# Splitting the first load of a streaming softmax into two transfers of 64 partitions

## The chip, the cores and the metric

The kernel runs on one core of a Trainium2 chip. The metric is device time in microseconds (us): lower is better. The core has the engines VectorE (DVE in the profile), ScalarE (ACT), GpSimd (POOL), TensorE (PE, not used here) and SyncE (SP), and 16 DMA engines that move data between DRAM and the on-chip memory SBUF, which has 128 partitions.

## The reference

A softmax over the last axis of a float32 tensor of 16 x 1024 x 512, that is, 16384 rows of 512 numbers, 33.55 MB in and 33.55 MB out.

```python
x_max = np.max(x, axis=-1, keepdims=True)
exp_x = np.exp(x - x_max)
return (exp_x / np.sum(exp_x, axis=-1, keepdims=True)).astype(np.float32)
```

## The kernel before

The 16384 rows are seen as 128 row sets of 128 rows, one row of each set in each partition. The row sets are moved in eight blocks of 16 (`BLOCKS`): block (0, 16) is the first 2048 rows of the input, and partition p takes 16 neighbouring rows of it, 32 KB in one piece of DRAM. So each of the eight loads ("L" in `ORDER`) and of the eight stores ("S") moves 4.19 MB over all 128 partitions. SBUF holds a ring of 96 row sets (`RING`), called `held`; the softmax is computed in place there.

Computing goes in 16 groups of eight row sets, two groups to a block. For each group g:

- VectorE takes the negated maximum of the eight rows of each partition (`rowmax`, M0 to M15 in the list `VECTOR`, line 164). Before the first group of a block it waits for the load's semaphore (`take(nc.vector, loaded[k], 16)`, through the helper on line 110). A transfer adds 16 to its semaphore when all of it has landed.
- ScalarE takes exp(x - max) of one row at a time and sums it (line 195, eight activations a group, in a loop over the groups). It preloads its table on line 188.
- VectorE takes reciprocals of the sums (line 170), and GpSimd (P0 to P11) or VectorE (V12 to V15) multiplies the rows by them (line 172).

Both the order of VectorE's steps (`VECTOR`) and the order of the transfers (`ORDER`) are written out by hand. All transfers are issued by SyncE, in the order of `ORDER`. The first six loads (`AHEAD`) are issued at once, without a wait (lines 124 to 136, through `load` on line 125). Behind them, SyncE waits for the two multiplies of a block before it stores it (line 152), and for the store of a block before it loads another one into its place in the ring. At the end SyncE waits for the last stores.

The program starts with an entry barrier of all engines (line 223 of a library file in the profile), and a second one stands between the six loads and the rest (line 137). When the program is finalized, `loads_at_the_head` moves the first load that SyncE issues from behind the entry barrier to ahead of it:

```python
AT_HEAD = {mybir.EngineType.SP: 1}
...
        loads = [
            i
            for i in body.instructions
            if i.engine == engine and type(i).__name__ == "InstDMACopy"
        ][:count]
...
        main.instructions[barrier:barrier] = loads
```

The count is in instructions: one DMA instruction of SyncE goes ahead of the barrier. In the list of the loads, that is all of load 0.

Of the kernel before, what the change touches and what calls it, by code (L numbers as in the profile page):

```python
# [1 line left out]

# [4 lines left out]

F32 = mybir.dt.float32
EXP = mybir.ActivationFunctionType.Exp
AX = mybir.AxisListType.X  # L10

GROUP = 8
GROUPS = 16
RING = 12 * GROUP

BLOCKS = [(0, 16), (16, 32), (32, 48), (48, 64), (64, 80), (80, 96), (96, 112), (112, 128)]
ORDER = [
    ("L", (0, 16)),
    ("L", (16, 32)),
    ("L", (32, 48)),
    ("L", (48, 64)),
    ("L", (64, 80)),
    ("L", (80, 96)),
    ("S", (0, 16)),
    ("S", (16, 32)),  # L30
    ("S", (32, 48)),
    ("L", (96, 112)),
    ("L", (112, 128)),
    ("S", (48, 64)),
    ("S", (64, 80)),
    ("S", (80, 96)),
    ("S", (96, 112)),
    ("S", (112, 128)),
]
AHEAD = 6  # L40

VECTOR = """
    M0 M1 P0 M2 P1 M3 P2 M4 P3 M5 P4 M6 P5 M7 P6 M8 P7 M9 P8 M10 P9 M11
    P10 M12 P11 M13 V12 M14 V13 M15 V14 V15
"""

AT_HEAD = {mybir.EngineType.SP: 1}

def loads_at_the_head(nc):

    main, body = nc.main_func.blocks[0], nc.main_func.blocks[1]
    for engine, count in AT_HEAD.items():
# [5 lines that stand above are left out]
        barrier = next(  # L62
            n
            for n, i in enumerate(main.instructions)
            if i.engine == engine and type(i).__name__ == "InstDrain"
        )
        for load in loads:
            body.instructions.remove(load)
        main.instructions[barrier:barrier] = loads


@with_exitstack
def kernel(
    ctx: ExitStack,
    tc: tile.TileContext,
    x: bass.AP,
    out: bass.AP,
):
    nc = tc.nc
    nc.at_finalize(loads_at_the_head)  # L80
    P = nc.NUM_PARTITIONS

    d = x.shape[-1]
    x_rows, out_rows = x.flatten_outer_dims(), out.flatten_outer_dims()
    assert x_rows.shape[0] == GROUPS * GROUP * P

    def in_dram(rows, a, b):

        first, last = next(k for k in BLOCKS if k[0] <= a and b <= k[1])
        block = rows[first * P : last * P].rearrange("(p r) d -> p r d", p=P)  # L90
        return block[:, a - first : b - first, :]

    held = nc.alloc_sbuf_tensor("held", [P, RING, d], F32).ap()
    shift = nc.alloc_sbuf_tensor("shift", [P, GROUPS * GROUP], F32).ap()
    sums = nc.alloc_sbuf_tensor("sums", [P, GROUPS * GROUP], F32).ap()
    recip = nc.alloc_sbuf_tensor("recip", [P, GROUPS * GROUP], F32).ap()

    loads = [k for what, k in ORDER if what == "L"]
    stores = [k for what, k in ORDER if what == "S"]
    loaded = {k: nc.alloc_semaphore(f"loaded{k[0]}") for k in loads}  # L100
    scaled = [nc.alloc_semaphore(f"scaled{g}") for g in range(GROUPS)]
    stored = {k: nc.alloc_semaphore(f"stored{k[0]}") for k in stores}
    maxed = nc.alloc_semaphore("maxed")
    expd = nc.alloc_semaphore("expd")
    to_pool = nc.alloc_semaphore("to_pool")
    to_vector = nc.alloc_semaphore("to_vector")

    def take(engine, semaphore, n):

        engine.wait_ge(semaphore, n).then_inc(semaphore, -n)  # L110

    def rows(a, b):
        assert a // RING == (b - 1) // RING
        return held[:, a % RING : (b - 1) % RING + 1, :]

    def meets(k, a, b):
        return k[0] < b and a < k[1]

    def group(g):
        return g * GROUP, (g + 1) * GROUP  # L120

    def stats(t, g):
        return t[:, g * GROUP : (g + 1) * GROUP]

    def load(k):
        copy = nc.sync.dma_start(out=rows(*k), in_=in_dram(x_rows, *k))
        copy.then_inc(loaded[k], 16)
        return copy

    with tc.manual_schedule():
        for _, k in ORDER[:AHEAD]:
            tc.no_tile_sem_insts.add(load(k).ins.name)
    tc.close()
    tc.compile()  # L137

    taken, done = set(), set()
    for what, k in ORDER[AHEAD:]:  # L140
        if what == "L":
            for s in stores:
                if meets(s, k[0] - RING, k[1] - RING) and s not in taken:
                    take(nc.sync, stored[s], 16)
                    taken.add(s)
            load(k)
        else:
            for g in range(GROUPS):
                if meets(k, *group(g)) and g not in done:
                    take(nc.sync, scaled[g], 1)  # L150
                    done.add(g)
            nc.sync.dma_start(out=in_dram(out_rows, *k), in_=rows(*k)).then_inc(
                stored[k], 16
            )


    seen = set()

    def rowmax(g):
        for k in loads:  # L160
            if meets(k, *group(g)) and k not in seen:
                take(nc.vector, loaded[k], 16)
                seen.add(k)
        nc.vector.reduce_max(  # L164
            out=stats(shift, g), in_=rows(*group(g)), axis=AX, negate=True
        ).then_inc(maxed, 1)

    def scale(g, engine, ready):
        take(nc.vector, expd, 1)
        nc.vector.reciprocal(out=stats(recip, g), in_=stats(sums, g)).then_inc(ready, 1)  # L170
        take(engine, ready, 1)
        engine.tensor_mul(  # L172
            out=rows(*group(g)),
            in0=rows(*group(g)),
            in1=stats(recip, g).unsqueeze(2).to_broadcast([P, GROUP, d]),
        ).then_inc(scaled[g], 1)

    for step in VECTOR.split():
        what, g = step[0], int(step[1:])
        if what == "M":  # L180
            rowmax(g)
        elif what == "V":
            scale(g, nc.vector, to_vector)
        else:
            scale(g, nc.gpsimd, to_pool)


    nc.scalar.preload_act_table(EXP)  # L188

    with nc.scalar.Fori(0, GROUPS) as i:  # L190
        take(nc.scalar, maxed, 1)
        for r in range(GROUP):
            row = held[:, bass.ds(i % (RING // GROUP) * GROUP + r, 1), :]
            at = bass.ds(i * GROUP + r, 1)
            act = nc.scalar.activation(  # L195
                out=row,
                in_=row,
                func=EXP,
                bias=shift[:, at],
                scale=1.0,  # L200
                accum_out=sums[:, at],
            )
        act.then_inc(expd, 1)


    for k in stores:
        if k not in taken:
            take(nc.sync, stored[k], 16)


# [1 line left out]
_INS = ['x']  # L212
_OUTS = [((16, 1024, 512), 'float32')]


# [23 lines left out]
```

## Time and profile before

| | |
|---|---|
| median of 3 runs | 160.07 us (159.98 to 160.23) |
| the profiled execution's own time | 160.14 us |
| its span, first to last instruction | 158.8 us |
| VectorE, ScalarE, GpSimd busy | 90.6, 92.0, 84.0 us |
| DMA queue of SyncE | 2304 packets, 67.11 MB |
| loads, issue to landing | 12.2 / 29.7 / 58.8 us (least, median, most) |
| stores, issue to landing | 17.9 / 28.3 / 38.3 us |

The profile is that of one execution. "Busy" is the time in which an engine executes; waits, and the issuing of transfers, are not counted. An answer by stages (windows) has, for each stretch of the span: its ends and length in us, the busy time of VectorE, ScalarE and GpSimd with the number of instructions, the clock granted to TensorE, the mean busy share of the 16 DMA engines, and GB/s. In the page's slices each digit is the busy share of one of 40 equal pieces of the span, in tenths. A row of the timeline has start and length in us, then engine, line and operation; "SPq" is SyncE's own instruction queue. A row of the waits has who waited for whom, us in total, how many times, and the longest.

### The profile page before, as it was taken

The page shows a single profiled execution, that of the slowest core. Times are in us where ns is not written, and L with a number is a line of the kernel's source. Part 1 is how long each engine was busy: PE and PEld are TensorE (multiplying, and loading weights), DVE is VectorE, ACT ScalarE, POOL GpSimd, SP SyncE. Part 2 cuts the span into 40 slices and gives each one's busy share as a digit, 9 for nine tenths or more (in the row PEclk, how much of TensorE's full clock was granted, in tenths as well). Part 3 has the DMA queues.
Part 4 walks back from the last instruction along what each step waited for, and adds up shares of the span by engine and source line. Part 5 has one row for each costly group of instructions (what it writes and reads, how often), then busy time and mean ns, then how long its engine had stood idle before and what let it go on. Part 6 is the DMA issues. An engine that isn't in the chain of part 4 may idle for free. (4 is left out here: it accounts for less than half of the span.)

```text
span 158.8 us, 747 instructions
## 1 busy us (share of the span) xinstructions
DVE 90.6 (57%) x36; ACT 92.0 (58%) x257; POOL 84.0 (53%) x16
## 2 busy tenths in 40 slices
DVE  0008959777977977887700000795999998640000
ACT  0300699999999999999993000059934929200000
POOL 0000009999999999999999999259200000000000
DMA  7999999999999998999999999999999999999996
GB/s 264 470 454 396 413 487 421 396 454 470 396 396 487 437 396 380 413 396 454 470 396 421 462 437 396 446 479 396 421 446 454 396 437 473 413 404 454 446 413 264
DMA packets 2305, 67.12 MB, mean 423 GB/s; under 512 B 256, under 2 KB 256, under 8 KB 256
## 3 DMA queue, kind: packets, MB, share of 16 engines
q1 hardware_dynamic: 2304, 67.11, 98.9%
q14 instruction: 1, 0.01, 0.0%
HBM read 33.55 MB, written 33.55 MB: 423 GB/s over the span
## 5 line engine op out<-in xcount | busy, mean ns | idle before, releaser
L195 ACT ACTIVATE held<-held,shift x128 | 90.3, 712 | 40.0 <-ACTq L110 40.0
L172 POOL TENSOR_TENSOR held<-held,recip 128x4096 f32<-128x4096 f32 x12 | 83.8, 7015 | 28.0 <-POOLq L110 28.0
L164 DVE TENSOR_REDUCE shift<-held 128x8 f32<-128x4096 f32 x16 | 70.3, 4399 | 33.2 <-DVEq L110 33.2
L195 ACT ACTIVATION_READ_ACCUMULATOR held<-held,shift x128 | 24.6, 192 | 0.0
L172 DVE TENSOR_TENSOR held<-held,recip 128x4096 f32<-128x4096 f32 x4 | 18.3, 4570 | 0.6
L170 DVE RECIPROCAL recip<-sums 128x8 f32<-128x8 f32 x16 | 3.2, 201 | 16.5 <-DVEq L110 16.5
L188 ACT ACT_TABLE_LOAD x1 | 1.3, 1283 | 3.9 <-PEq L137 3.9
L223 POOL MEMSET const-float32-0.0<- 128x1 f32 x1 | 0.1, 98 | 0.2 <-issue 0.2
L223 POOL MEMSET const-uint8-127<- 128x1 uint8 x1 | 0.1, 102 | 0.0
L223 POOL MEMSET const-bfloat16-1.0<- 128x1 bf16 x1 | 0.1, 101 | 0.0
L223 POOL MEMSET const-float32-1.0<- 128x1 f32 x1 | 0.1, 98 | 0.0
## 6 DMA issues: line engine op xcount, KB each, us to landing
held<-in_x_dram SPq DMA_DIRECT2D x8, 4096.0 KB, 29.7
out_dram<-held SPq DMA_DIRECT2D x8, 4096.0 KB, 28.3
```

The costliest lines, as they stand in the source:

```text
L164: nc.vector.reduce_max(out=stats(shift, g), in_=rows(*group(g)), axis=AX, negate=True).then_inc(maxed, 1)
L170: nc.vector.reciprocal(out=stats(recip, g), in_=stats(sums, g)).then_inc(ready, 1)
L172: engine.tensor_mul(out=rows(*group(g)), in0=rows(*group(g)), in1=stats(recip, g).unsqueeze(2).to_broadcast([P, GROUP, d]),).then_inc(scal ...
L188: nc.scalar.preload_act_table(EXP)
L195: act = nc.scalar.activation(out=row, in_=row, func=EXP, bias=shift[:, at], scale=1.0, accum_out=sums[:, at],)
L223: nc = _bacc.Bacc("TRN2", target_bir_lowering=False, num_devices=1)
```

## The change

Load 0 becomes two transfers, the first of partitions 0 to 63, the second of partitions 64 to 127. Both move the same 32 KB per partition as before and add 16 each to the same semaphore, and VectorE's wait for load 0 is for 32. As one instruction of SyncE is moved ahead of the entry barrier, it is the first of the two; the second one follows behind the barrier, ahead of loads 1 to 5. The other transfers, the ring and the orders stay.

```diff
+FIRST = [slice(0, 64), slice(64, 128)]
...
+    def parts(k):
+        return FIRST if k == ORDER[0][1] else [slice(None)]
+
     def load(k):
-        copy = nc.sync.dma_start(out=rows(*k), in_=in_dram(x_rows, *k))
-        copy.then_inc(loaded[k], 16)
-        return copy
+        copies = []
+        for part in parts(k):
+            copy = nc.sync.dma_start(out=rows(*k)[part], in_=in_dram(x_rows, *k)[part])
+            copies.append(copy.then_inc(loaded[k], 16))
+        return copies
...
         for _, k in ORDER[:AHEAD]:
-            tc.no_tile_sem_insts.add(load(k).ins.name)
+            for copy in load(k):
+                tc.no_tile_sem_insts.add(copy.ins.name)
...
-                take(nc.vector, loaded[k], 16)
+                take(nc.vector, loaded[k], 16 * len(parts(k)))
```

## The prediction

> **What bounds the kernel now.** I read the page's span, slices and DMA totals first, to see which resource has no spare time.
>
> ```profile
> span 158.8 us, 747 instructions
> ...
> DVE 90.6 (57%) x36; ACT 92.0 (58%) x257; POOL 84.0 (53%) x16
> ...
> DMA  7999999999999998999999999999999999999996
> ...
> DMA packets 2305, 67.12 MB, mean 423 GB/s; under 512 B 256, under 2 KB 256, under 8 KB 256
> ...
> q1 hardware_dynamic: 2304, 67.11, 98.9%
> ```
>
> No compute engine is busy for 60% of the span; the 16 DMA engines are busy for 98.9% of it. So the kernel is a stream of 67.1 MB, and whatever lengthens that stream lengthens the run. The packets say how it is cut: 256 are tiny (16 transfers x 16 DMA engines, one closing mark each), so 2048 carry data, 67.1 MB / 2048 = 32.77 KB each. That is one partition's 16 rows of 512 floats. Each 4.19 MB transfer is 128 such packets, eight to a DMA engine.
>
> Next the stages, to get a packet's duration. In a stage, packets = GB/s x us / 32.77 KB, and packet time = DMA share x 16 x us / packets. A packet counts where it starts, so a share can exceed 1.
>
> ```profile
> 0.00:1.00 1.00, 0.00 (x0) 0.00 (x0) 0.20 (x4) 1.00 0.00 0
> 1.00:2.00 1.00, 0.00 (x0) 0.00 (x0) 0.00 (x0) 1.00 1.83 524
> 2.00:3.00 1.00, 0.00 (x0) 0.00 (x0) 0.00 (x0) 1.00 0.31 131
> 3.00:4.00 1.00, 0.00 (x0) 0.07 (x1) 0.00 (x0) 1.00 0.93 393
> ...
> 12.00:36.00 24.00, 19.52 (x8) 18.89 (x53) 12.54 (x2) 1.00 1.01 434
> ...
> 142.00:157.00 15.00, 0.00 (x0) 0.00 (x0) 0.00 (x0) 1.00 1.02 439
> ```
>
> From 12 to 36 us only loads are in flight: 318 packets in 387.8 engine-us, 1.22 us each. From 142 to 157 us only stores are: 201 packets in 244.8, 1.22 us each. The first microsecond of data is different: 16 packets start between 1 and 2 us, one per DMA engine, and last 1.83 us each on average. Nothing moves before 1 us.
>
> Last the SyncE queue at the head, the waits, and the end.
>
> ```profile
> 0.00 3.13 SPq L126 DMA_DIRECT2D held<-in_x_dram  x6
> ```
>
> ```profile
> DVE shift L164 <- DVEq L110: 33.2, 2, 20.8
> ...
> ACT L188 <- PEq L137: 3.9, 1, 3.9
> ```
>
> ```profile
> 12.33 4.42 DVE L164 TENSOR_REDUCE shift<-held 128x8 f32<-128x4096 f32 x1 [12.33 <-DVEq L110]
> ```
>
> ```profile
> 136.38 4.43 DVE held L172
> ```
>
> SyncE issues all six first loads in 3.13 us, and they keep the DMA engines fed to about 60 us (1 + 6 x 9.76). VectorE's first reduce starts when load 0 has landed, at 12.33 us. VectorE's last multiply ends at 140.81, while the DMA engines have work to the end of the span 18 us later. The last store is 9.76 of these, so about 8 us of cover lies between compute and the DMA queue at the end.
>
> **The change, part by part.** The sum is made against the profiled execution, 160.14 us (span 158.8 and 1.34 around it), which lies 0.07 above the median of 160.07.
>
> *One more issue on SyncE.* Load 0 becomes two instructions. Issues last 0.33 to 0.49 us (the rows of L126), so loads 1 to 5 and the drain behind them move back by up to 0.49. Loads 1 to 5 are hidden by what is queued: half a load is four packets per DMA engine, 4 x 1.22 = 4.9 us of work, against a second half that SyncE can issue at 0.79 us as it issued load 1 before. Without that cover the 0.79 us of the barrier would come on top. ScalarE's table load waits for that drain (3.93 us) and would end near 5.7, far ahead of its first use at 17.1: nothing.
>
> *The first issue is shorter or not.* It names 64 partitions instead of 128 and took 0.38 us. From nothing saved to half of it: 0 to -0.19; I take -0.1, no row being nearer to either end.
>
> *Sixteen more closing marks*, one per DMA engine. The q1 queue held each engine for 0.989 x 158.8 = 157.1 us; 128 x 1.22 = 156.2 are data and 16 marks share what is left with the long first packets, so one costs at most 0.9/16 = 0.06 us. I take 0.05.
>
> *VectorE's wait goes from 16 to 32.* It is the same instruction on the same semaphore; behind it stand M0 and all of VectorE's order, and ScalarE and GpSimd behind M0. They get load 0 when its second half lands. A later landing moves the computing along with the DMA stream, and the 8 us of cover at the end stay.
>
> *Which partitions are written at one time.* This is the term that decides. Before, 16 DMA engines write into all 128 partitions at once. After, the first transfer's 64 packets all go to partitions 0 to 63, then the second's 64 to partitions 64 to 127. No row shows a transfer over fewer than 128 partitions, so I bound it. Lower end: each DMA engine is limited by itself, a packet stays at 1.22 us, 0. Upper end: the limit is at the doors through which data enter SBUF, spread over the partitions; two engines then share a door, a packet takes 2.44 us, and load 0's eight packets per engine cost 8 x 1.22 = 9.76 us more. Two readings draw me to the upper end. Loads and stores have the same 1.22 us, though one reads DRAM and the other writes it, so the limit is not DRAM's; it is in the DMA engine or on the SBUF side. And when all 16 engines start together their packets stretch to 1.83 us, so engines do hold each other up at some common place. That is weak evidence on the place, but it is the nearest row there is, and 1.83 is half of the way to 2.44.
>
> [...]
>
> *What softens the term.* Two things at the head. The long first packets hold 1.83 - 1.22 = 0.61 us that may lie beside the doubled time instead of on top. And engines that start up to 1 us apart do not share a door all of the time. Together 0 to about -1.6; I take the 0.6 of the first, which has a row.
>
> Sum: 9.76 - 0.6 - 0.1 + 0.05 = +9.1, from 160.07 to **169.2 us**. By itself this case spans 167.9 (softened by 1.6 and by 0.19, near enough) to 170.4 (9.76, an exposed issue, a mark).
>
> **The rivals.**
>
> *One of two sharing engines goes first.* If a door serves one engine's packet fully before the other's, the first one passes to the other half early and the two separate: the late one loses four packets, 4 x 1.22 = 4.9, not eight. 165.0 us. The steady 1.22 us in every stage speaks for even service, so this is the lesser form.
>
> *Packets are not slowed at all.* The DMA engine itself is the limit. For: 1.22 us in both directions, as one engine's fixed pace would give. Against: the stretched first packets. Time: 160.07 - 0.1 + 0.05 = 160.0, no change.
>
> *A faster start, the other side.* The first 16 packets lose 0.61 us each, in the very time in which SyncE issues load 0 and the loads behind it. If that is the handing out of 128 rows, 64 rows are handed out sooner: 0.1 to 0.6 us, some 159.6 us. It decides only if the half transfers cost under about 0.3 us, because it can never exceed 0.61 + 0.19.
>
> *Each half on half of the DMA engines.* If 64 partitions are served by the eight engines that serve them now, the rate stays, but the second eight start with the second issue, 0.79 us late, and the end goes by them: 160.9 us. The 256 closing marks (16 per transfer) show that every transfer uses 16 engines now; none shows what a half does.
>
> [...]
>
> **How the numbers follow.** About 0.2% (0.3 us) is what a measurement of this kernel can tell from no change. Chances: the doubled packet 0.77, one engine first 0.07, no change 0.08, a faster start 0.03, eight engines each 0.03, four to a door 0.02. The predicted time is the first one's. To hold 8 in 10 the range takes all of it and reaches down to the second, 164.6 (165.0 less some softening) to 170.4. Slower: 0.77 + 0.07 + 0.03 + 0.02 = 0.89; same 0.08; faster 0.03.
>
> **What would show it.** If right: between 2 and 20 us the DMA rate is near 217 GB/s at a DMA share of 1, so packets of 2.4 us, and 434 after that; VectorE's first reduce starts near 21.5 instead of 12.33; every later step is later by the same 9 us, with DMA share 1.00 in the middle; ScalarE's table load moves by at most 0.5 us. Packets of 1.22 us from 4 us on, with a first reduce near 12.3, would prove the main term wrong. A rate of 217 with a share of 0.5 would mean that engines stand idle, not that they share a door. If the head is later by 9 us and the end is not, some cover later in the stream was overlooked.

## The result and the profile after

The changed kernel takes 170.15 us (median of 5 runs, 170.04 to 170.29) against 160.02 us (159.95 to 160.23) for the kernel before, measured beside it. The ratio is 1.0627, with a 95% interval of 1.0615 to 1.0638: 10.1 us slower. The profiled execution took 170.29 us, with a span of 169.0.

The page of the changed kernel, its span, slices and DMA totals:

```profile
span 169.0 us, 748 instructions
...
DMA  8999989999999999999999999999999999999995
GB/s 202 209 209 209 202 334 434 434 434 434 434 434 434 434 419 450 419 450 419 450 419 450 419 442 427 442 427 442 419 450 419 434 396 467 403 458 403 465 403 256
DMA packets 2321, 67.12 MB, mean 397 GB/s; under 512 B 272, under 2 KB 272, under 8 KB 272
...
q1 hardware_dynamic: 2320, 67.11, 98.5%
```

Read the first five slices (4.2 us each). The DMA row says 8 or 9, so the engines are as busy as ever, but the GB/s row says 202 to 209 where the rest of the span has about 434. Busy time alone would have hidden the whole loss. The tiny packets are 272, that is, 16 more closing marks for one more transfer.

The stages of the same kernel (ends, length, compute, clock, DMA share, GB/s):

```profile
4.00:20.00 16.00, 0.00 (x0) 1.28 (x1) 0.00 (x0) 1.00 1.03 213
24.00:60.00 36.00, 29.61 (x12) 32.08 (x91) 25.73 (x4) 1.00 1.01 434
```

From 4 to 20 us, 213 GB/s x 16 us / 32.77 KB = 104 packets start, in 1.03 x 16 x 16 = 264 engine-us: **2.54 us a packet**. From 24 us on it is 1.22 again. Only load 0 is slow.

The timeline at its first reduce and its last multiply, SyncE's queue at the head, and the waits:

```profile
0.00 4.21 SPq L134 DMA_DIRECT2D held<-in_x_dram  x7
```

```profile
23.14 8.74 DVE L173 TENSOR_REDUCE shift<-held 128x8 f32<-128x4096 f32 x2 [23.14 <-DVEq L113]
...
146.51 4.42 DVE L181 TENSOR_TENSOR held<-held,recip 128x4096 f32<-128x4096 f32 x1
```

```profile
DVE shift L173 <- DVEq L113: 43.3, 2, 23.1
...
ACT L197 <- PEq L146: 5.0, 1, 5.0
```

VectorE's first reduce starts at 23.14 us instead of 12.33, 10.8 later; its last multiply starts at 146.51 instead of 136.38, 10.1 later, and the span ends 10.2 later. The wait for load 0 has taken it: 23.1 us, the longest of the two waits in the row above, against 12.33. (The row's total, 43.3 us against 33.2, has a second wait in it, which fell from 20.8 to 20.2.)

### The profile page after: what moved, and what is told of

Its sections match the earlier page's. It is cut to its first block, busy times and chain, and to the rows that moved or that the text cites. A ratio compares the mean times of both kernels' runs of the same rounds, so it can differ in the third digit from the quotient of the medians.

```text
span 169.0 us, 748 instructions
## 1 busy us (share of the span) xinstructions
DVE 90.6 (54%) x36; ACT 92.0 (54%) x257; POOL 84.0 (50%) x16
## 3 DMA queue, kind: packets, MB, share of 16 engines
q1 hardware_dynamic: 2320, 67.11, 98.5%
## 5 line engine op out<-in xcount | busy, mean ns | idle before, releaser
L173 DVE TENSOR_REDUCE shift<-held 128x8 f32<-128x4096 f32 x16 | 70.3, 4398 | 43.3 <-DVEq L113 43.3
L204 ACT ACTIVATION_READ_ACCUMULATOR held<-held,shift x128 | 24.0, 187 | 0.0
```

The costliest lines, as they stand in the source:

```text
L173: nc.vector.reduce_max(out=stats(shift, g), in_=rows(*group(g)), axis=AX, negate=True).then_inc(maxed, 1)
L204: act = nc.scalar.activation(out=row, in_=row, func=EXP, bias=shift[:, at], scale=1.0, accum_out=sums[:, at],)
```

## The experiments

The theory after the result is the prediction's: the limit is on SBUF's side and goes by which partitions are written at one time. The expectations call this the doors; a door, and two engines sharing one, is the author's assumption, and no run shows it. Rivals: the split or the barrier itself costs; the narrow piece of DRAM is slow; small transfers are slow. Every kernel below starts from the changed one; "ratio" is its time over that of the kernel before, measured beside it, with the 95% interval behind it.

### Split, but over all partitions

```diff
-FIRST = [slice(0, 64), slice(64, 128)]
+FIRST = [(slice(None), slice(0, 8)), (slice(None), slice(8, 16))]
```

> Load 0 in two transfers again, one ahead of the barrier and one behind it, but each over all 128 partitions with 8 of the 16 rows (16 KB pieces). Doors theory (two DMA engines share a door into SBUF when only 64 neighbouring partitions are written): all doors are in use, packets of 16 KB take about 0.61 us, the time is that of before, 159.9 to 160.4 us, first reduce near 12.3 us. Rival, splitting or the second issue behind the barrier is what costs: about 170 us again.

160.09 us against 160.18, ratio 0.9993 (0.9974 to 1.0012). Two transfers, one of them behind the barrier, 16 more marks: no price that this can tell. Its stages and first reduce:

```profile
4.00:12.00 8.00, 0.00 (x0) 1.28 (x1) 0.00 (x0) 1.00 1.08 461
```

```profile
12.41 8.74 DVE L173 TENSOR_REDUCE shift<-held 128x8 f32<-128x4096 f32 x2 [12.41 <-DVEq L113]
```

### Both halves ahead of the barrier

```diff
-AT_HEAD = {mybir.EngineType.SP: 1}
+AT_HEAD = {mybir.EngineType.SP: 2}
```

> Both half loads of 64 partitions ahead of the entry barrier. Doors theory: the barrier plays no part, 169.9 to 170.4 us with packets of 2.55 us. Rival, the cost is the second half's waiting behind the barrier: back to about 160 us.

170.16 us, ratio 1.0597 (1.0557 to 1.0637), first reduce at 23.25 us. The barrier has no part in it.

### Quarters and eighths

```diff
-FIRST = [slice(0, 64), slice(64, 128)]
+FIRST = [slice(32 * i, 32 * i + 32) for i in range(4)]     # quarters
+FIRST = [slice(16 * i, 16 * i + 16) for i in range(8)]     # eighths
```

> Load 0 in four transfers of 32 neighbouring partitions. [...] Rival, a transfer slows in proportion to the partitions it spans: packets of about 5 us, load 0 takes about 40 us, the time is 189 to 192 us.

> Load 0 in eight transfers of 16 neighbouring partitions. [...] Rival in proportion to the partitions: packets of about 10 us, about 230 us. Rival, any transfer under 128 partitions has one fixed lower rate: 170 to 171 us.

Quarters: 169.78 us, ratio 1.0575 (1.0536 to 1.0614). From 4 to 20 us their packets last 2.53 us each (201 and 197 GB/s in the halves of that stretch, at a share of 0.96: 97 packets in 246 engine-us). Halving the partitions again costs nothing more, so here the price does not follow their number. Eighths: 185.77 us, ratio 1.1572 (1.1513 to 1.1632). The stages of the eighths:

```profile
4.00:12.00 8.00, 0.00 (x0) 1.28 (x1) 0.00 (x0) 1.00 1.14 131
```

131 GB/s x 8 us / 32.77 KB = 32 packets in 1.14 x 128 = 146 engine-us: 4.56 us each. So 64 and 32 neighbours went at one rate (2.54 and 2.53 us a packet), and 16 neighbours at another, a little over half as high (2.54 / 4.56 = 0.56).

### DRAM or SBUF

The next two separate the ends. Eight transfers again; one end takes 16 neighbours, the other one in eight. Each changes where the first 2048 rows land and leave, as its expectation says.

```diff
+FIRST = [(slice(16 * i, 16 * i + 16), slice(i, 128, 8)) for i in range(8)]   # SBUF near, DRAM far
+FIRST = [(slice(i, 128, 8), slice(16 * i, 16 * i + 16)) for i in range(8)]   # SBUF far, DRAM near
...
-            copy = nc.sync.dma_start(out=rows(*k)[part], in_=in_dram(x_rows, *k)[part])
+            to, of = part if isinstance(part, tuple) else (part, part)
+            copy = nc.sync.dma_start(out=rows(*k)[to], in_=in_dram(x_rows, *k)[of])
```

> Load 0 in eight transfers, each into 16 neighbouring partitions, but from every eighth 32 KB piece of the 4.19 MB in DRAM (so the first 2048 rows land in other partitions, and leave in another order). Doors into SBUF: as with 16 neighbouring partitions before, packets of 4.54 us and about 185.8 us. Rival, the narrow stretch of DRAM is what slows the half transfers: packets of 1.2 to 2.6 us, 160 to 171 us.

> The mirror: eight transfers, each into every eighth partition, from 16 neighbouring 32 KB pieces of DRAM (the first 2048 rows land in other partitions, and leave in another order). [...] Rival, DRAM: 4.5 us packets and about 186 us. Rival, doors that are taken in the order of the partitions, eight neighbours to a door: packets of 1.2 us and about 160 us.

SBUF near, DRAM far: 185.44 us, ratio 1.1577 (1.1554 to 1.16), as the eighths. SBUF far, DRAM near: 169.92 us, ratio 1.0608 (1.0587 to 1.063), as the halves. The stages of the one and of the other:

```profile
4.00:12.00 8.00, 0.00 (x0) 1.28 (x1) 0.00 (x0) 1.00 1.14 131
12.00:20.00 8.00, 0.00 (x0) 0.00 (x0) 0.00 (x0) 1.00 1.14 131
```

```profile
4.00:12.00 8.00, 0.00 (x0) 1.28 (x1) 0.00 (x0) 1.00 0.94 197
12.00:20.00 8.00, 0.00 (x0) 0.00 (x0) 0.00 (x0) 1.00 0.96 197
```

Same number of transfers, same bytes, 16 partitions each; the rate goes by where in SBUF they lie (4.56 us a packet against 2.53), and DRAM's end changes nothing that these times tell (185.44 us against 185.77 for the eighths). In the second kernel 197 GB/s x 16 us / 32.77 KB = 96 packets in (0.94 + 0.96) x 128 = 243 engine-us, 2.53 us. The other rival, eight neighbours to a door, would have given 1.2 us here. Why 16 partitions that lie eight apart go at the rate of 64 neighbours is not shown.

### Elsewhere in the stream, and out of SBUF

```diff
-        return FIRST if k == ORDER[0][1] else [slice(None)]
+        return FIRST if k == ORDER[3][1] else [slice(None)]     # load 3 instead of load 0
+        return FIRST if k == ORDER[-1][1] else [slice(None)]    # for the last store alone
...
```

For the last store, the edit also issues every load whole again, issues a store in its parts, and lets SyncE wait at the end for 16 per part.

> Load 0 whole again; load 3, which is issued behind the barrier and read from about 31 to 41 us, in two halves of 64 neighbouring partitions. Doors: the same price in the middle of the stream, packets of 2.55 us in it, 8 x (2.55 - 1.21) = 10.7 us more, 170.0 to 171.0 us. Rival, the price belongs to the head of the kernel: 160.0 to 160.5 us.

> Load 0 whole again; the last store in two transfers of 64 neighbouring partitions. If the doors are also what limits reading from SBUF: packets of about 2.4 to 2.6 us in the last store, 169.5 to 171.0 us. If only writes into SBUF are held: 160.0 to 160.5 us.

Load 3 in halves: 170.13 us, ratio 1.0628 (1.0609 to 1.0647). The price is the same in the middle of the stream (2.56 and 2.51 us a packet from 32 to 48 us), with VectorE, ScalarE and GpSimd computing beside it:

```profile
20.00:30.00 10.00, 6.99 (x5) 10.00 (x30) 6.29 (x1) 1.00 1.02 442
32.00:40.00 8.00, 5.94 (x3) 8.00 (x25) 8.00 (x2) 1.00 0.96 197
40.00:48.00 8.00, 4.69 (x3) 8.00 (x24) 8.00 (x2) 1.00 1.04 217
```

The last store in halves: 168.55 us, ratio 1.0525 (1.0507 to 1.0543). Reading from SBUF is slowed in the same way, to 2.37 and 2.50 us a packet from 150 to 164 us:

```profile
140.00:147.00 7.00, 0.84 (x1) 0.00 (x0) 0.00 (x0) 1.00 1.02 440
150.00:157.00 7.00, 0.00 (x0) 0.00 (x0) 0.00 (x0) 1.00 0.97 215
157.00:164.00 7.00, 0.00 (x0) 0.00 (x0) 0.00 (x0) 1.00 0.94 197
```

Its price is 8.4 us, and the time is 1 to 2.5 below what was expected. Its trace has packets of 1.2 to 2.1 us where one transfer follows another; that some engines are then still in one half and others already in the next is the author's reading of them. The packets make up nearly the whole price: its page has the queue busy for 98.8% of 167.2 us, that is, 165.2 us for each engine against 157.1 before, 8.1 more, where eight packets of 2.55 us would have made 10.6.

### Both halves in flight together

```diff
-            copy = nc.sync.dma_start(out=rows(*k)[part], in_=in_dram(x_rows, *k)[part])
+            queue = nc.scalar if part == FIRST[1] else nc.sync
+            copy = queue.dma_start(out=rows(*k)[part], in_=in_dram(x_rows, *k)[part])
```

> The second half of load 0 is issued by ScalarE instead of SyncE, behind the barrier, so both halves are in flight together and each DMA engine takes packets from two queues. Doors, if the 16 engines keep step with each other and are all in the same half at a time: packets of 2.55 us and about 170 us again. Doors, if the engines part, so that some write the lower half and others the upper: packets nearer to 1.21 us, 160.5 to 165 us. Rival, a half transfer is slow by itself whatever else is in flight: load 0 lands near 23 us and the end is near 170 us.

171.8 us (median of four runs, 170.14 to 173.41), ratio 1.0685 (1.063 to 1.074), worked out without the longest. The profiled execution is that longest one, so its lines show what the packets did there; that the other three runs went the same way is not shown. Its stages:

```profile
4.00:12.00 8.00, 0.00 (x0) 1.28 (x1) 0.00 (x0) 1.00 0.99 213
12.00:20.00 8.00, 0.00 (x0) 0.00 (x0) 0.00 (x0) 1.00 1.01 197
20.00:24.00 4.00, 0.00 (x0) 0.00 (x0) 0.00 (x0) 1.00 0.77 131
```

In the trace the engines keep step: nearly all of them take a lower-half packet, then nearly all an upper-half one, 2.3 to 2.6 us each. When the lower half is done, load 1's packets take its turns; upper-half packets beside them last about 3.2 us, and load 0 lands later still (first reduce at 29.51 us). The engines did not part, and a second queue does not help. This kernel does not refute the rival that a half transfer is slow by itself; the next one does.

### The even partitions, then the odd ones

```diff
-FIRST = [slice(0, 64), slice(64, 128)]
+FIRST = [slice(0, 128, 2), slice(1, 128, 2)]
```

> [...]

Each transfer has 64 partitions, as in the changed kernel, but no two neighbours. 160.48 us, ratio 1.0023 (1.0013 to 1.0033). Its stages and first reduce:

```profile
4.00:12.00 8.00, 0.00 (x0) 1.28 (x1) 0.00 (x0) 1.00 1.04 446
```

```profile
12.49 8.74 DVE L173 TENSOR_REDUCE shift<-held 128x8 f32<-128x4096 f32 x2 [12.49 <-DVEq L113]
```

This is the changed kernel with nothing altered but which 64 partitions go together: two transfers of 64 partitions, one ahead of the barrier and one behind. Of the 10.1 us, about 9.7 are gone, and 0.37 (0.0023 x 160.2) are left. Packets are 1.22 us (446 GB/s x 8 us / 32.77 KB = 109 packets in 1.04 x 128 = 133 engine-us), as in the kernel before. So a transfer of 64 partitions is not slow by itself, nor is one that covers half of SBUF's partitions; it depends on which half. How the partitions are dealt to the engines is not shown.

The remaining 0.37 us goes with a longer first issue. SyncE's queue at the head, before, then here:

```profile
0.00 0.38 SPq L126 DMA_DIRECT2D held<-in_x_dram  x1
```

```profile
0.00 0.55 SPq L134 DMA_DIRECT2D held<-in_x_dram  x1
```

Stages cut finer show when the first data move, before and here:

```profile
1.00:1.30 0.30, 0.00 (x0) 0.00 (x0) 0.00 (x0) 1.00 5.20 1420
```

```profile
1.00:1.30 0.30, 0.00 (x0) 0.00 (x0) 0.00 (x0) 1.00 0.00 0
1.30:2.00 0.70, 0.00 (x0) 0.00 (x0) 0.00 (x0) 1.00 2.27 655
```

Thirteen engines have begun their first packet by 1.3 us before; here none has. The first packets start at 1.01 us and at 1.33, and the changed kernel (0.55 us, 1.34) does as this one. The packets hold an engine no longer than before (98.7% of 159.1 us, 157.0 us, against 157.1), so a later start is what is left. But the first reduce is only 0.16 later (12.49 us against 12.33), and the two kernels above that leave load 0 whole have it at 12.38 and 12.57; that the issue accounts for all of the 0.37 is not shown.

## Why the prediction was right

170.15 us lies in the range of 164.6 to 170.4, on the forecast side and 0.95 above the forecast of 169.2. Of the cause it is shown that the rate goes with the SBUF end and with which partitions are together (2.54 us a packet for 64 neighbours, 1.22 for 64 alternate ones), not with their number alone, the split, the barrier, the place in the stream or DRAM. What in the hardware makes it so is not shown.

- **The main term, 9.76 us, was too small.** It took a shared packet at twice 1.22. The profile shows 2.54, so 8 x (2.54 - 1.22) = 10.6. That two engines share a door, each at half its rate, was the author's assumption; measured is a packet a little more than twice as long.
- **The softening, -0.6, was there, and larger.** The stages of the changed kernel at its start, and where load 1 follows:

```profile
1.00:2.00 1.00, 0.00 (x0) 0.00 (x0) 0.00 (x0) 1.00 1.03 262
2.00:3.00 1.00, 0.00 (x0) 0.00 (x0) 0.00 (x0) 1.00 1.06 262
3.00:4.00 1.00, 0.00 (x0) 0.00 (x0) 0.00 (x0) 1.00 1.28 262
...
20.00:22.00 2.00, 0.00 (x0) 0.00 (x0) 0.00 (x0) 1.00 0.75 213
```

Eight packets start between 1 and 2 us and last 2.06 us each, eight between 2 and 3, 2.12 each, and the next eight last 2.56. So an engine's first packet took 2.09 us, 0.26 more than the 1.83 before, and not 2.54 - 1.22 = 1.32 more. That softens the term by 1.06: load 0's packets held an engine 9.5 us longer.
- **Load 1's first packets had no term.** The 13 packets that start between 20 and 22 us are the first of load 1, and last 1.85 us each instead of 1.22, while late engines still write the upper half. By the packet records of the trace this is 0.6 us for each engine.
- **The first issue, -0.1, had the wrong sign.** An instruction for 64 partitions took 0.55 us, not less than 0.38, and the first packets began 0.33 later; the average engine began 0.5 later (1.78 us against 1.26), as the stages above show eight of the 16 starting after 2 us. The bound "from nothing saved to half of it" left out that a smaller transfer can be dearer to issue. What the issue alone costs is open: the quarters, issued in 0.39 us, end 0.37 us below the halves, but the kernel with partitions eight apart, issued in 0.58, ends 0.23 below them too.
- **The marks, 0.05,** are too small to be seen, as the split over all partitions shows.
- **The covers held.** Loads 1 to 5 were never late, and VectorE's last multiply ends 18.1 us before the end of the span; it was 18.0. The table load starts 1.1 us later (5.0 against 3.9), not at most 0.5: the longer first issue counts, too, and the issues behind it. It still ends 21.6 us ahead of its first use.
- **"Every later step by the same 9 us" was wrong by 0.7.** The head is 10.8 late, the end 10.1. Of the 10.8, 9.5 are load 0's packets and 0.5 the start; the rest lies between the ends of the packets and the landing, and why is open. Load 4 is still 10.7 late, load 5 only 10.0. Before, the stream has a dent at 57 to 61 us, when the last of the six loads ends; the changed kernel has none, there or at the end of its own six loads ten microseconds later. The stages of before, then of after (57 to 61, and 67 to 71):

```profile
57.00:61.00 4.00, 4.00 (x2) 4.00 (x13) 4.00 (x2) 1.00 1.02 344
```

```profile
57.00:61.00 4.00, 3.94 (x1) 4.00 (x12) 4.00 (x1) 1.00 1.07 459
67.00:71.00 4.00, 3.34 (x2) 4.00 (x13) 4.00 (x2) 1.00 1.11 475
```

In the trace of before, load 5 lands 10.4 us after load 4, against 9.7 for the others. The 42 packets that start in the dent last 1.55 us each, which holds an engine 42 x (1.55 - 1.22) / 16 = 0.9 us longer. The dent is in every kernel here whose six loads end near 61 us (369 GB/s in the split over all partitions, 270 with even and odd ones), and in none where they end ten or more later. Its cause is open.

The page's q1 rows close the account. Before, 98.9% of 158.8 us is 157.1 us of packets for each engine; after, 98.5% of 169.0 is 166.5, 9.4 more. Load 0 makes 9.5 of that, load 1's first packets 0.6, the missing dent -0.9, and 0.2 are spread over the stream. The later start adds 0.5, and 0.3 more lies in how far apart the engines end: 10.2 us, the difference of the two spans.

So the main term was right in kind, and the nearness of the sum is in part luck. Against the forecast of +9.1, what was too small or had no term makes 2.5 us (0.8 of the doubled packet, 0.6 of load 1, 0.6 of the start, 0.5 of the last two), and what was missing on the other side makes 1.4 (0.5 of softening and the dent).

**One reading was no evidence.** The 1.83 us of the first 16 packets was taken to show that engines hold each other up. The kernel with even and odd partitions has the same long start, although its packets are 1.22 us from 4 us on: 459 GB/s and a share of 1.59 between 1 and 2 us, 14 packets of 1.82 us.

```profile
1.00:2.00 1.00, 0.00 (x0) 0.00 (x0) 0.00 (x0) 1.00 1.59 459
```

The stretch goes with the start, before and here; it is no sign of engines that hold each other up. The other reading, equal rates in both directions, pointed the right way but could not have told a limit on SBUF's side from an engine's own; the experiments can.

**The rivals.** Packets not slowed: refuted by 2.54 us. A faster start: the start is later. One engine first: service was even, with every packet from 4 to 20 us at 2.4 to 2.6 in the packet records. Each half on eight engines: a half lands 16 marks, and 16 packets run at a time. Four to a door: four times 1.22 us would be 4.9, and no packet of load 0 lasted over 2.6; with 16 neighbours it was 4.56 us a packet, which cost 25.6 us.

No kernel here beats the one before; the split over all partitions equals it.

## What to carry to other kernels

When a kernel is bound by DMA, look at which partitions one transfer covers, not only at its size: here 64 neighbours ran at half the rate (213 GB/s against 434), 64 alternate ones at the full rate (446). The halved rate showed in GB/s beside an unchanged DMA share (1.03 against 1.01), so read the two together and work out the time of a packet. To get a first piece earlier, cut along the rows and keep all the partitions in each piece: that cost nothing here (160.09 us against 160.18), though no run computes on such a piece.

## What the runs showed of the hardware

- A packet of 32.77 KB took 1.22 us where load 0 covered all 128 partitions or 64 alternate ones, 2.54 where it covered 64 neighbours, 2.53 with 32 neighbours or with 16 that lie eight apart, and 4.56 with 16 neighbours. Why the steps are a little over twice and a little under four times 1.22 is open.
- A store out of SBUF was slowed by 64 neighbours as a load into it was (2.37 and 2.50 us a packet in the two stages of the halved last store).
- The issue of a first transfer took 0.38 or 0.39 us for 128 partitions and for 16 or 32 neighbours, and 0.55 to 0.58 for 64, neighbours or not, and for 16 that lie eight apart. With 64, data began to move 0.3 us later (1.33 and 1.34 us against 1.01).
